# The first stage of a two-block transformer kernel: late convolutions re-ordered, ScalarE and VectorE work pinned behind evictions, the layer norm put between other products, and modulation products moved to the feed-forward stage

## The chip, the cores and the metric

One Trainium2 chip, the program on one core. The metric is the device time of one execution in microseconds (us), the median of three runs.

## What is computed

Two blocks over 512 tokens of width 1024, in float32 accuracy. Only the first stage of the first block, its layer norm and the start of its feed-forward part matter here:

```python
def first_block(x, ...):
        h = rmsnorm(x, norm1_g[l])
        z = h @ w_in[l] + b_in[l]
        z_glu, z_rx, z_rg, z_ga, z_gb = jnp.split(z, split_idx, axis=-1)

        u = z_glu[..., :D_CONV] * jax.nn.sigmoid(z_glu[..., D_CONV:])
        u = causal_depthwise_conv(u, conv_dw_w[l], conv_dw_b[l])     # 31 taps
        u = jax.nn.silu(layernorm(u, conv_ln_g[l], conv_ln_b[l]))
        y_a = u @ conv_w_out[l] + conv_b_out[l]

        xb = causal_depthwise_conv(z_rx, lru_conv_w[l], lru_conv_b[l])   # 4 taps
        hb = rg_lru(xb, lru_wa[l], lru_ba[l], lru_wx[l], lru_bx[l], lru_lambda[l])
        y_b = (hb * jax.nn.gelu(z_rg, approximate=True)) @ lru_w_out[l]

        m = jax.nn.sigmoid(z_ga) * y_a + jax.nn.sigmoid(z_gb) * y_b
        x = x + m @ w_mix_out[l]
        h = rmsnorm(x, norm2_g[l])
        x = x + (jax.nn.silu(h @ ffn_w1[l]) * (h @ ffn_w3[l])) @ ffn_w2[l]
```

Beside it a vector c is turned into 72 modulation columns for the second block, `silu(c) @ w_ada` (w_ada is 72 tiles of 128 x 1024).

## The kernel before

Activations lie channels on partitions, tokens along the free axis: a tensor of width 1024 is eight tiles of 128 x 512. **Products.** Every float32 operand is split in two (high and low part), and each K tile of a product is three matmuls, high x high, low x high, high x low (`mm3`, L132, L133, L134). A product of K = 1024 is 24 matmuls, one of K = 1280 is 30. Weights land by DMA from SyncE's queue in a ring of five `st` tiles; ScalarE copies a tile to `whi` (L125), VectorE, or GpSimd for some, subtracts it to `wlo` (L126); both have rings of five. Products land in a ring of three PSUM tiles `mm`, which must be evicted before the fourth product on starts; sums over partitions and convolution accumulators use a second PSUM ring of five, `ax`.

**Order of the work.** The program is a list of steps in one order, and every engine runs its instructions in the order in which the steps wrote them, save that a scheduler moves an instruction to where its inputs are expected. The first stage's steps are
g0 r0 r1 r2 r3 r4 g1 g2 a0 r5 a1 g3 a2 r6 a3 g4 a4 r7 r8 s0 g5 r9 b0 g6 b1 b2 g7 b3 b4 q0 q1 s1 q2 ... q9:
g are the gated-unit tiles (two products, `ga` evicted at L421 and `th` at L430 by ScalarE), r the recurrence's inputs, a and b its two gate products (`gt`, L545), s its scan, q the gelu gates (`ge`, then split to `hbh` and `hbl`). Then come eight pairs z_m, y_m (`yb_step`: a gate `thb` and a product over `hbh`), ga0 to ga7 (gates `tha`), ya0 to ya7 (products over the layer norm's output `u2h`, `u2l`) and the mixer's mx0 to mx7, and the feed-forward part.

g0 and r0 to r4 run before the normalised input is there: their products use the raw input, and VectorE multiplies the result by the norm's factor (`raw_z`, L395). What follows them, the 31-tap convolution of g0 and `rest` of r0 to r4 (three 4-tap products `xb`, L406, and a split to `xbh`, `xbl`), is kept in a list `late` and written when `norm_h(6)` has made the normalised input.

The 31-tap convolution is VectorE work in the background: taps d = 0 and 1 are ScalarE copies that start two PSUM accumulators (L401, L403, L404), the other 29 are VectorE multiply-adds (L406 `ax<-th,d_hdw,ax`); `total` joins the two (L446, L447), GpSimd adds up the channel sum `lnm` (L479). `later` queues such pieces in `bg` with a cost, `runbg` writes them after a step as far as that step's slack allows, and a NEXT mark ends its turn. The layer norm is queued the same way (`ln_push`): mean (L196, L224, L634), subtraction and squares (L639, L252), the inverse root (L232, L200 to L202, L217), output (L646, L647 and a split). What is still queued after ga7 is written there at once (`flush`).

An `ada_step` multiplies one w_ada tile with c and sums it up (VectorE, L327); its 512 KB come through the same `st` ring. Of the 72, 4 are written after y products, 8 after ga, 6 after ya, and the others during the first feed-forward part at a rate of 1.0 a product (`ada_between`).

`NKEEP` limits how many split weight tiles of a product are kept for its second token half.

Of the kernel before, what the change touches and what calls it, by code (L numbers as in the profile page):

```python
# [16 lines left out]
ALU = mybir.AluOpType  # L17
# [36 lines left out]
def build(tc, I, O, dbg=None):  # L54
# [11 lines left out]
    LA_D, LA_P = 4, 4  # L66
    NKEEP = {"w_mix_out": 3, "w_out": 3, "ffn_w2": 2}
    uid = [0]
# [263 lines left out]
    H = {}  # L332
# [30 lines left out]
    def behind(hold):  # L363
        return tc.issue_after(H["h_last"]) if hold else nullcontext()

    late = []

    def norm_h(m0):
        def fn(W):
            if m0 == 0:  # L370
                nc.gpsimd.dma_start(crow, I["c_2"].partition_broadcast(P))
                H["h"] = pairs(KT)
            ts = []
            for m in (m0, m0 + 1):
                t = at(n="ht")
                V.scalar_tensor_tensor(t, X[m], col("norm1_g", m), H["R"], ALU.mult, ALU.mult)
                act(H["h"][m][0], t, AF.Copy)
                ts.append(t)
            for m in (m0, m0 + 1):
                h, l = H["h"][m]  # L380
                H["h_last"] = V.tensor_tensor(l, ts[m - m0], h, ALU.subtract).ins
            if m0 + 2 == KT:
                for f in late:
                    f()
                late[:] = [None]
        return fn

    def raw_end(W):
        del H["xg"], H["R"]

    def raw_z(W, t):

        ps = pmm()
        gemm(ps, W, H["xg"])
        V.tensor_tensor(t, ps, H["R"], ALU.mult)  # L395
        return t
# [11 lines left out]
    CV = [None] * KT  # L408
    EV = [None]

    def glu_step(m, raw=False):
# [11 lines left out]
        def fg(W):  # L423
# [3 lines left out]
            else:  # L427
                pg = pmm()
                gemm(pg, W, H["h"])
            act(u, pg, AF.Tanh, bias=dcol["hb_in"][:, 8 + m:9 + m], scale=0.5)  # L430
            V.scalar_tensor_tensor(u, u, 1.0, st["a"], ALU.add, ALU.mult)
            cv = {}

            def taps(d0, d1):
                def f():
                    if d0 == 0:
                        cv["p"] = [pax(), pax()]
                    for d in range(d0, d1):
                        w = dcol["hdw"][:, m * 31 + 30 - d:m * 31 + 31 - d]
                        acc = cv["p"][d % 2]  # L440
                        delay(acc, u, d, w, col("conv_dw_b", m), first=d < 2)
                return f

            def total():
                CV[m] = at(n="cv")
                act(CV[m], cv["p"][0], AF.Copy)  # L446
                V.tensor_tensor(CV[m], CV[m], cv["p"][1], ALU.add)  # L447
# [37 lines left out]
    def rx_step(j, raw=False):  # L485
# [19 lines left out]
        def rest(z, xb, hold=False):  # L505
# [5 lines left out]
            def parts():  # L511
                XBP[j] = (at(F32R, "xbh"), at(F32R, "xbl"))
                split(xb, *XBP[j])

# [21 lines left out]
    def gate_step(g, m):  # L536
        j = g * 5 + m
        def fn(W):
            (hi, lo, kc), = W
            for q, nmq in ((0, "hba"), (1, "hbx")):  # L540
# [3 lines left out]
                th = at(n="gt")  # L544
                act(th, pg, AF.Tanh, bias=dcol[nmq][:, j:j + 1], scale=0.5)  # L545
                GT[q, j] = th
# [6 lines left out]
            V.scalar_tensor_tensor(tt, a2, 1.0, tt, ALU.add, ALU.mult)  # L553
            V.scalar_tensor_tensor(XB[j], ith, 1.0, XB[j], ALU.add, ALU.mult)
            GT[2, j] = tt
# [19 lines left out]
    def rg_step(j):  # L575
        def fn(W):
            pz = pmm()
            gemm(pz, W, H["h"])
            ge = at(n="ge")
            EV[0] = act(ge, pz, AF.Gelu_apprx_tanh, bias=col("b_in", 26 + j))  # L580
            V.tensor_tensor(ge, ge, XB[j], ALU.mult)

            def parts():
                HB[j] = (at(F32R, "hbh"), at(F32R, "hbl"))
                split(ge, *HB[j])
            defer(2, parts)
        add(wunits("w_in", 26 + j, KT, [8]), fn, own=1.4)

    pool_steps = [0, 0]
    for it in ("g0 r0 r1 r2 r3 r4 g1 g2 a0 r5 a1 g3 a2 r6 a3 g4 a4 r7 r8 s0 g5 r9 b0 g6 b1 b2 g7 b3 b4 "  # L590
               "q0 q1 s1 q2 q3 q4 q5 q6 q7 q8 q9").split():
        n = int(it[1])
        if it in ("g0", "r0", "r1", "r2", "r3", "r4"):
            {"g": glu_step, "r": rx_step}[it[0]](n, raw=True)
            if it in ("r1", "r2", "r3"):
                for m in {"r1": (0, 2), "r2": (4,), "r3": (6,)}[it]:
                    add([], norm_h(m), own=2.9 + (12.0 if m == 6 else 0.0))
            if it == "r4":
                pool_steps[0] = len(steps)
                add([], raw_end)  # L600
            continue
# [5 lines left out]
    def yb_step(m):  # L607
        st = {}

        def fz(W):  # L610
            pz = pmm()
            gemm(pz, W, H["h"])
            th = at(n="thb")
            act(th, pz, AF.Tanh, bias=dcol["hb_in"][:, 44 + m:45 + m], scale=0.5)
            st["th"] = th
# [8 lines left out]
        add(wunits("lru_w_out", m, NRNN, [5, 5]), fy, own=0.6)  # L624
        if m % 2:
            ada_step()

# [23 lines left out]
    def ln_push(W):  # L651
        bg.extend([NEXT, NEXT])
        later(0.9, ln_mean)
# [3 lines left out]
        for m in range(KT):  # L657
            later(1.4, lambda m=m: ln_out(m))

    for m in range(KT):  # L660
        yb_step(m)
# [5 lines left out]
    def ga_step(m):  # L667
        def fn(W):
            pz = pmm()
            gemm(pz, W, H["h"])  # L670
            TA[m] = at(n="tha")
            act(TA[m], pz, AF.Tanh, bias=dcol["hb_in"][:, 36 + m:37 + m], scale=0.5)
        add(wunits("w_in", 36 + m, KT, [8]), fn)
        ada_step()

    def ya_step(m):
# [11 lines left out]
        add(wunits("conv_w_out", m, KT, [8]), fn, own=2.1)  # L688
        if m < 6:
            ada_step()  # L690

# [225 lines left out]
    def ada_between():  # L917
        H["ada"] = H.get("ada", 0.0) + 1.0
        while H["ada"] >= 1.0:
# [695 lines left out]
    for i, (units, fn, slack) in enumerate(steps):  # L1615
# [16 lines left out]
        elif i < front[0]:  # L1632
            runbg(slack - spent[0])
        else:
# [83 lines left out]
```

## Time and profile before

| | |
|---|---|
| median of three runs | 2270.68 us (2270.66 to 2271.85) |
| profiled execution, its own time | 2268.78 us |
| its span, first to last instruction | 2267.1 us |
| mean granted TensorE clock | 0.991 |
| PE (TensorE) busy | 2207.7 us, 97% |
| DVE (VectorE) busy | 1401.8 us, 62% |
| ACT (ScalarE) busy | 941.8 us, 42% |
| POOL (GpSimd) busy | 159.3 us, 7% |

The profile is of one execution. "Idle before" a group is the time in which its engine did nothing, and after the arrow stands the instruction that ended it. The granted clock is 1.00 at 2.4 GHz and 0.50 at 1.2 GHz.

### The profile page before, as it was taken

The page shows a single profiled execution, that of the slowest core. Times are in us where ns is not written, and L with a number is a line of the kernel's source. Part 1 is how long each engine was busy: PE and PEld are TensorE (multiplying, and loading weights), DVE is VectorE, ACT ScalarE, POOL GpSimd, SP SyncE. Part 2 cuts the span into 40 slices and gives each one's busy share as a digit, 9 for nine tenths or more (in the row PEclk, how much of TensorE's full clock was granted, in tenths as well). Part 3 has the DMA queues.
Part 4 walks back from the last instruction along what each step waited for, and adds up shares of the span by engine and source line. Part 5 has one row for each costly group of instructions (what it writes and reads, how often), then busy time and mean ns, then how long its engine had stood idle before and what let it go on. Part 6 is the DMA issues. An engine that isn't in the chain of part 4 may idle for free.

```text
span 2267.1 us, 29984 instructions
## 1 busy us (share of the span) xinstructions
PE 2207.7 (97%) x11688; PEld 1888.2 (83%) x11688; DVE 1401.8 (62%) x2349; ACT 941.8 (42%) x1517; POOL 159.3 (7%) x179
## 2 busy tenths in 40 slices
PE   8899999699999999999999999999999999999997
PEld 6687788588888899988889987888888899988887
DVE  7999996768555448433325768675656558433334
ACT  6566433443222235322224567573433445322232
POOL 3334330000000000000100011000000000000000
PEclk9999999799999999999999999999999999999999
DMA  5433347245656534423234431213222323423342
GB/s 191 118 92 122 101 134 225 82 144 174 203 195 192 150 103 149 131 94 102 86 102 129 161 96 57 66 47 103 66 75 75 117 89 96 147 95 98 92 121 66
DMA packets 81438, 265.54 MB, mean 117 GB/s; under 512 B 10208, under 2 KB 12512, under 8 KB 81296
## 3 DMA queue, kind: packets, MB, share of 16 engines
q1 hardware_dynamic: 79888, 262.64, 36.8%
q8 instruction: 92, 1.51, 0.3%
q0 software_dynamic: 1264, 0.69, 0.1%
q14 instruction: 50, 0.41, 0.1%
q10 hardware_dynamic: 144, 0.29, 0.0%
HBM read 255.13 MB, written 4.19 MB: 114 GB/s over the span
## 4 chain that ended last, share of the span: by engine, by line
PE 81%; DVE 11%; issue 1%; ACT 1%; DMA 0%; POOL 0%; DVEq 0%; ACTq 0%; POOLq 0%
PE mm L132 24%; PE mm L133 24%; PE mm L134 24%; DVE ax L406 3%; DVE wlo L126 1%; PE ax L1231 1%; PE ax L1232 1%; PE ax L1233 1%; PE ax L1286 1%; PE ax L224 1%; PE ax L1415 1%; DVE xb L406 1%; PE ax L196 1%; DVE xb L567 1%; DMA st<-w_ada 0%
## 5 line engine op out<-in xcount | busy, mean ns | idle before, releaser
L125 ACT ACTIVATE whi<-st 128x1024 fp32r<-128x1024 f32 (+3 forms) x420 | 427.1, 1018 | 959.3 <-PE mm L133 594.4
L126 DVE TENSOR_TENSOR wlo<-st,whi 128x1024 fp32r<-128x1024 f32 (+3 forms) x378 | 454.1, 1202 | 415.8 <-ACT whi L125 414.7
L132 PE MATMUL mm<-pfh,whi 128*128 128x512 f32 (+1 forms) x1676 | 568.9, 339 | 0.5 <-ACT sq L251 0.5
L133 PE MATMUL mm<-pfl,whi 128*128 128x512 f32 (+1 forms) x1676 | 565.6, 338 | 0.0
L134 PE MATMUL mm<-pfh,wlo 128*128 128x512 f32 (+1 forms) x1676 | 564.4, 337 | 1.2 <-DVE wlo L126 1.2
L134 PEld LDWEIGHTS mm<-pfh,wlo 128*128 128x128 f32 x1676 | 316.8, 189 | 34.0 <-DVE wlo L126 1.9
L132 PEld LDWEIGHTS mm<-pfh,whi 128*128 128x128 f32 x1676 | 317.2, 189 | 33.5 <-ACT sq L251 1.4
L133 PEld LDWEIGHTS mm<-pfl,whi 128*128 128x128 f32 x1676 | 317.1, 189 | 31.7 <-issue 0.5
L132 PE MATMUL mm<-hi,whi 128*128 128x512 f32 x464 | 183.0, 394 | 10.4 <-ACT hi L354 6.2
L133 PE MATMUL mm<-lo,whi 128*128 128x512 f32 x464 | 183.4, 395 | 1.3 <-DVE lo L355 1.3
L134 PE MATMUL mm<-hi,wlo 128*128 128x512 f32 x464 | 182.4, 393 | 0.4 <-DVE wlo L126 0.4
L132 PE MATMUL mm<-mh,whi 128*128 128x256 f32 (+1 forms) x528 | 176.7, 335 | 2.2 <-ACT mh L852 1.1
L133 PE MATMUL mm<-ml,whi 128*128 128x256 f32 (+1 forms) x528 | 176.9, 336 | 0.0
L134 PE MATMUL mm<-mh,wlo 128*128 128x256 f32 (+1 forms) x528 | 176.4, 334 | 0.0
L406 DVE SCALAR_TENSOR_TENSOR ax<-th,d_hdw,ax 128x508 f32<-128x508 f32 (+27 forms) x232 | 157.7, 729 | 1.1 <-ACT ax L401 0.2
L133 PE MATMUL mm<-m1l,whi 128*128 128x512 f32 x368 | 143.3, 390 | 0.2 <-DVE m1l L686 0.2
L134 PE MATMUL mm<-m1h,wlo 128*128 128x512 f32 x368 | 143.0, 389 | 0.0
L132 PE MATMUL mm<-m1h,whi 128*128 128x512 f32 x368 | 143.0, 389 | 0.0
L327 DVE SCALAR_TENSOR_TENSOR st<-st,crow 128x1024 f32<-128x1024 f32 x72 | 88.5, 1229 | 73.6 <-DMA st<-w_ada 73.5
L865 DVE TENSOR_TENSOR fs<-fs,mm 128x512 f32<-128x512 f32 (+1 forms) x75 | 45.0, 600 | 128.0 <-PE mm L134 127.7
L132 PEld LDWEIGHTS mm<-hi,whi 128*128 128x128 f32 x464 | 88.1, 190 | 29.6 <-ACT hi L354 6.2
L132 PEld LDWEIGHTS mm<-mh,whi 128*128 128x128 f32 x528 | 100.1, 190 | 13.1 <-ACT mh L852 1.5
(363 smaller groups left out, 3319.2 us busy)
## 6 DMA issues: line engine op xcount, KB each, us to landing
st<-w_gu SPq DMA_DIRECT2D x102, 512.0 KB, 3.5
st<-w_ada SPq DMA_DIRECT2D x72, 512.0 KB, 4.0
st<-ffn_w SPq DMA_DIRECT2D x56, 512.0 KB, 3.6
st<-w_in SPq DMA_DIRECT2D x51, 512.0 KB, 4.0
st<-w2fm SPq DMA_DIRECT2D x51, 512.0 KB, 3.5
st<-w_dn SPq DMA_DIRECT2D x38, 448.0 KB, 3.3
st<-w_dn SPq DMA_DIRECT2D x24, 512.0 KB, 3.6
st<-w2v SPq DMA_DIRECT2D x16, 512.0 KB, 3.5
```

The source lines that it names most:

```text
L125: h = act(hi, src, AF.Copy)
L126: (eng or V).tensor_tensor(lo, src, hi, ALU.subtract)
L132: mm(out, whi, xh, start=start, stop=False)
L133: mm(out, whi, xl, start=False, stop=False)
L134: block[0] = mm(out, wlo, xh, start=False, stop=stop)
L196: mm(pc[:, i * nt + j:i * nt + j + 1], acc[:, r[0] + P * j:r[0] + P * (j + 1)], ones1, start=True, stop=True)
L224: mm(R[:, :nt * P], ones, dg.rearrange("p n t -> p (n t)"), start=True, stop=True)
L327: V.scalar_tensor_tensor(w, w, 1.0, crow, ALU.mult, ALU.mult, accum_out=mods[:, n:n + 1])
L406: V.scalar_tensor_tensor(acc[:, d:], u[:, :T - d], w, acc[:, d:], ALU.mult, ALU.add)
L567: V.tensor_tensor_scan(XB[j], GT[0, j], XB[j], 0.0, ALU.mult, ALU.add)
L865: V.tensor_tensor(s, s, rs(st["u"], r), ALU.mult)
L1231: mm(o, h[:, sl], hi[c], start=k == 0, stop=False)
```

## The change

1. `NKEEP` loses `w_mix_out` and has 8 instead of 3 for `w_out`, the product at the end of the second block's mixer.
2. `norm_h(6)` writes three late pieces (conv of g0, rest of r0, r1); those of r2, r3 and r4 are written in `raw_end`, behind r4's VectorE multiplication (`z_last`).
3. The convolution's ScalarE taps, `total` and the splits to `xbh` and `hbh` are pinned behind the last gate activation (`EV`), its VectorE taps behind the last gate multiplication but one (`DV`). `CV[m]` uses u's tile again. The last `hb` split is deferred by one step instead of two.
4. Stated costs: 5.0 instead of 12.0 for `norm_h(6)`, 7.0 for `raw_end`, a factor of 1.15 on the background from z0 on, and one NEXT less before the layer norm.
5. `ada_step`: none in the y and ga stages, 8 instead of 6 in ya, and 1.2 a product in the feed-forward part.

```diff
-    NKEEP = {"w_mix_out": 3, "w_out": 3, "ffn_w2": 2}
+    NKEEP = {"w_out": 8, "ffn_w2": 2}
...
+    NEARLY = 3
     late = []
...
             if m0 + 2 == KT:
-                for f in late:
+                for f in late[:NEARLY]:
                     f()
-                late[:] = [None]
+                del late[:NEARLY]
         return fn
 
     def raw_end(W):
         del H["xg"], H["R"]
+        H["h_last"] = H["z_last"]
+        for f in late:
+            f()
+        late[:] = [None]
 
     def raw_z(W, t):
...
-        V.tensor_tensor(t, ps, H["R"], ALU.mult)
+        H["z_last"] = V.tensor_tensor(t, ps, H["R"], ALU.mult).ins
         return t
...
+    DV = [None, None]
+
+    def behind_ev():
+        return tc.issue_after(EV[0].ins) if EV[0] is not None else nullcontext()
+
+    def behind_dv():
+        return tc.issue_after(DV[0].ins) if DV[0] is not None else nullcontext()
+
+    def dv(ins):
+        DV[:] = [DV[1], ins]
...
-            act(u, pg, AF.Tanh, bias=dcol["hb_in"][:, 8 + m:9 + m], scale=0.5)
-            V.scalar_tensor_tensor(u, u, 1.0, st["a"], ALU.add, ALU.mult)
+            EV[0] = act(u, pg, AF.Tanh, bias=dcol["hb_in"][:, 8 + m:9 + m], scale=0.5)
+            dv(V.scalar_tensor_tensor(u, u, 1.0, st["a"], ALU.add, ALU.mult))
...
-                        delay(acc, u, d, w, col("conv_dw_b", m), first=d < 2)
+                        with behind_ev() if d < 2 else behind_dv():
+                            delay(acc, u, d, w, col("conv_dw_b", m), first=d < 2)
...
-                CV[m] = at(n="cv")
-                act(CV[m], cv["p"][0], AF.Copy)
+                CV[m] = u
+                with behind_ev():
+                    act(u, cv["p"][0], AF.Copy)
...
-                split(xb, *XBP[j])
+                with behind_ev():
+                    act(XBP[j][0], xb, AF.Copy)
+                V.tensor_tensor(XBP[j][1], xb, XBP[j][0], ALU.subtract)
...
-            defer(2, parts)
+            defer(2 if j < NRNN - 1 else 1, parts)
...
-                    add([], norm_h(m), own=2.9 + (12.0 if m == 6 else 0.0))
+                    add([], norm_h(m), own=2.9 + (5.0 if m == 6 else 0.0))
             if it == "r4":
                 pool_steps[0] = len(steps)
-                add([], raw_end)
+                add([], raw_end, own=7.0)
...
         add(wunits("lru_w_out", m, NRNN, [5, 5]), fy, own=0.6)
-        if m % 2:
-            ada_step()
...
     def ln_push(W):
-        bg.extend([NEXT, NEXT])
+        bg.append(NEXT)
...
         add(wunits("w_in", 36 + m, KT, [8]), fn)
-        ada_step()
...
         add(wunits("conv_w_out", m, KT, [8]), fn, own=2.1)
-        if m < 6:
-            ada_step()
+        ada_step()
...
     def ada_between():
-        H["ada"] = H.get("ada", 0.0) + 1.0
+        H["ada"] = H.get("ada", 0.0) + 1.2
...
         elif i < front[0]:
-            runbg(slack - spent[0])
+            runbg((slack - spent[0]) * (1.15 if i >= yb0 else 1.0))
```

The built programs have the same number of instructions on every engine (PE 11378, DVE 2275, ACT 1442, POOL 179 rows, 571 DMAs on SP). The order differs at the places of points 2 to 5; of point 1 no row of any engine differs. Lines of the change are shifted by 5 to 19 against those of before (L395 is L400, L406 is L411, L421 is L436, L430 is L445, L634 is L653).

**VectorE around r4's multiplication** (`rx<-mm,R`, the eviction that frees r4's PSUM tile). `xb_355`, `xb_391`, `xb_460`, `xb_504` are the taps of r0 to r3. Before:

```order
L406 SCALAR_TENSOR_TENSOR xb_355<-rx_354,pcol,xb_355 128x509
L406 SCALAR_TENSOR_TENSOR xb_391<-rx_390,pcol,xb_391 128x509
L406 SCALAR_TENSOR_TENSOR xb_460<-rx_459,pcol,xb_460 128x511
L406 SCALAR_TENSOR_TENSOR xb_504<-rx_503,pcol,xb_504 128x511
L406 SCALAR_TENSOR_TENSOR xb_460<-rx_459,pcol,xb_460 128x510
L406 SCALAR_TENSOR_TENSOR xb_504<-rx_503,pcol,xb_504 128x510
L406 SCALAR_TENSOR_TENSOR xb_460<-rx_459,pcol,xb_460 128x509
L406 SCALAR_TENSOR_TENSOR xb_504<-rx_503,pcol,xb_504 128x509
L395 TENSOR_TENSOR rx_559<-mm_561,R_249 128x512
```

and now:

```order
L411 SCALAR_TENSOR_TENSOR xb_355<-rx_354,pcol,xb_355 128x509
L411 SCALAR_TENSOR_TENSOR xb_391<-rx_390,pcol,xb_391 128x509
L400 TENSOR_TENSOR rx_553<-mm_555,R_249 128x512
L411 SCALAR_TENSOR_TENSOR xb_460<-rx_459,pcol,xb_460 128x511
L411 SCALAR_TENSOR_TENSOR xb_504<-rx_503,pcol,xb_504 128x511
L411 SCALAR_TENSOR_TENSOR xb_460<-rx_459,pcol,xb_460 128x510
L411 SCALAR_TENSOR_TENSOR xb_504<-rx_503,pcol,xb_504 128x510
```

The six taps of r2 and r3 have gone from ahead of the eviction to behind it.

**ScalarE around the evictions of g1 and g2** (`ga`, `th`) and the first gate a0 (`gt`). Before:

```order
L421 ACTIVATE ga_619<-mm_620,pcol 128x512
L125 ACTIVATE whi_749<-st_557 128x1024
L125 ACTIVATE xbh_670<-xb_560 128x512
L125 ACTIVATE whi_787<-st_596 128x1024
L430 ACTIVATE th_674<-mm_675,d_hb_in 128x512
L401 ACTIVATE ax_1047<-th_674,pcol,d_hdw 128x512
L421 ACTIVATE ga_720<-mm_721,pcol 128x512
L430 ACTIVATE th_755<-mm_756,d_hb_in 128x512
L545 ACTIVATE gt_800<-mm_793,d_hba 128x512
```

and now:

```order
L436 ACTIVATE ga_611<-mm_612,pcol 128x512
L531 ACTIVATE xbh_650<-xb_460 128x512
L125 ACTIVATE whi_690<-st_501 128x512
L531 ACTIVATE xbh_654<-xb_504 128x512
L531 ACTIVATE xbh_658<-xb_554 128x512
L445 ACTIVATE th_662<-mm_663,d_hb_in 128x512
L125 ACTIVATE whi_749<-st_551 128x1024
L125 ACTIVATE whi_787<-st_596 128x1024
L436 ACTIVATE ga_720<-mm_721,pcol 128x512
L445 ACTIVATE th_755<-mm_756,d_hb_in 128x512
L564 ACTIVATE gt_800<-mm_793,d_hba 128x512
```

g1's `th` stands ahead of the two weight copies now, and the first tap of g1's convolution (L401) no longer stands ahead of g2's `ga`. The same kind of move is at b1: on VectorE the three taps of r9 (`xb_1392` before, `xb_1391` now), behind which ScalarE's split and the `ga` of g6 queue, were mixed with seven convolution taps, and now follow one another 26 rows earlier.

**The layer norm's mean.** VectorE at the end of the convolutions before, in the ga stage (`st,mods` is an `ada_step`, `cv<-cv,ax` the last convolution's total):

```order
L327 SCALAR_TENSOR_TENSOR st_3437,mods<-st_3437,crow 128x1024
L126 TENSOR_TENSOR wlo_3399<-st_3209,whi_3398 128x1024
L327 SCALAR_TENSOR_TENSOR st_3479,mods<-st_3479,crow 128x1024
L126 TENSOR_TENSOR wlo_3441<-st_3252,whi_3440 128x1024
L447 TENSOR_TENSOR cv_3241<-cv_3241,ax_2949 128x512
L634 TENSOR_SCALAR s_3286<-ax_3281 128x4
```

there, now:

```order
L411 SCALAR_TENSOR_TENSOR ax_2857<-th_1675,d_hdw,ax_2857 128x482
L126 TENSOR_TENSOR wlo_3047<-st_2917,whi_3046 128x1024
L464 TENSOR_TENSOR th_1675<-th_1675,ax_2858 128x512
L126 TENSOR_TENSOR wlo_3083<-st_2967,whi_3082 128x1024
L653 TENSOR_SCALAR s_3120<-ax_3115 128x4
L217 TENSOR_TENSOR dg_3122<-ident,s_3120 128x512
```

and TensorE now, where the mean's sums (L196) and its broadcast (L224) stand at the end of ga3 (`mm_3088`) and in ga4 (`mm_3151`):

```order
L134 MATMUL mm_3088<-hi_435,wlo_2960 128x512
L196 MATMUL ax_3115<-ones,lnm_1593 128x1 x4
L132 MATMUL mm_3151<-hi_421,whi_2963 128x512
L133 MATMUL mm_3151<-lo_422,whi_2963 128x512
L134 MATMUL mm_3151<-hi_421,wlo_2964 128x512
L132 MATMUL mm_3151<-hi_423,whi_2963 128x512
L133 MATMUL mm_3151<-lo_424,whi_2963 128x512
L134 MATMUL mm_3151<-hi_423,wlo_2964 128x512
L132 MATMUL mm_3151<-hi_425,whi_2963 128x512
L224 MATMUL ax_3124<-dg_3122,ones 128x512
```

Before, all four of the norm's statistics products (two L196, two L224) stood alone behind ga7's last matmul. Now the squares' sums stand behind 13 matmuls of ga6, the second broadcast 13 matmuls later, behind 2 of ga7, and the 22 others of ga7 stand between it and the first product over `u2h`. On ScalarE the table load for Silu moves from the copy of c (L326, in q9) to the first layer norm output (L647, now L666); both programs have 14 table loads.

## Rows read from the trace of the kernel before

**Rows 1.** The waits of TensorE over the first 460 us: who waited <- for what: us in total, times, longest us.

```profile
PE ax L196 <- DVE lnv L252: 9.7, 1, 9.7
...
PE mm L132 <- ACT ga L421: 5.0, 2, 2.8
```

**Rows 2.** Busy time of each engine in a stretch of 50 us (PE, PEld, DVE, ACT, POOL with instructions), then the granted clock, the DMA share and GB/s.

```profile
300.00:350.00 50.00, 50.00 (x222) 41.42 (x221) 47.78 (x68) 15.73 (x21) 14.12 (x9) 1.00 0.51 163
```

**Rows 3.** TensorE's timeline, the instructions that had to wait in the first stage: start us, us, engine, line, operation, out<-in, and in brackets the idle time before with what ended it.

```profile
67.74 0.73 PE L132 MATMUL mm<-hi,whi 128*128 128x512 f32 x1 [3.75 <-DVE rx L395]
...
82.00 0.50 PE L132 MATMUL mm<-xbh,whi 128*128 128x512 f32 x1 [1.50 <-ACT th L430]
...
85.86 0.50 PE L132 MATMUL mm<-xbh,whi 128*128 128x512 f32 x1 [2.19 <-ACT ga L421]
...
176.64 0.50 PE L132 MATMUL mm<-xbh,whi 128*128 128x512 f32 x1 [2.77 <-ACT ga L421]
...
267.40 0.50 PE L133 MATMUL mm<-hbl,whi 128*128 128x512 f32 x1 [2.26 <-DVE hbl L126]
```

**Rows 4.** VectorE's timeline ahead of the first of these waits.

```profile
55.89 11.20 DVE L406 SCALAR_TENSOR_TENSOR xb<-rx,pcol,xb 128x511 f32<-128x511 f32 x12
67.01 0.68 DVE L395 TENSOR_TENSOR rx<-mm,R 128x512 f32<-128x512 f32 x1
```

**Rows 5.** Three stretches in the columns of rows 2: behind the waits at 67.74, at 176.64 and through the layer norm.

```profile
67.80:71.20 3.40, 3.40 (x8) 2.68 (x9) 3.32 (x6) 3.40 (x7) 0.00 (x0) 0.51 0.00 0
...
177.10:180.50 3.40, 3.40 (x10) 2.62 (x9) 3.40 (x6) 3.37 (x8) 2.97 (x3) 0.50 0.80 160
...
402.40:426.20 23.80, 8.69 (x21) 6.10 (x22) 18.59 (x40) 11.85 (x20) 0.00 (x0) 0.50 0.06 22
```

**Rows 6.** ScalarE's timeline ahead of the waits at 85.86 and at 176.64.

```profile
84.42 0.78 ACT L401 ACTIVATE ax<-th,pcol,d_hdw 128x512 f32<-128x512 f32 x1 [2.47 <-DVE th L431]
85.14 0.67 ACT L421 ACTIVATE ga<-mm,pcol 128x512 f32<-128x512 f32 x1
...
174.44 0.63 ACT L125 ACTIVATE xbh<-xb 128x512 fp32r<-128x512 f32 x1 [9.09 <-DVE xb L406]
174.98 1.04 ACT L125 ACTIVATE whi<-st 128x1024 fp32r<-128x1024 f32 x1
175.92 0.67 ACT L421 ACTIVATE ga<-mm,pcol 128x512 f32<-128x512 f32 x1
```

**Rows 7.** TensorE's timeline: the first matmuls of ga0 (353.67), of ga4 (375.43) and of mx0 (467.32), and between the last two the layer norm's statistics products and the first product over its output.

```profile
353.67 0.39 PE L132 MATMUL mm<-hi,whi 128*128 128x512 f32 x1
...
375.43 0.39 PE L132 MATMUL mm<-hi,whi 128*128 128x512 f32 x1
...
398.59 1.05 PE L196 MATMUL ax<-ones,lnm 128*128 128x1 f32 x8 [1.23 <-POOL lnm L479]
...
400.62 1.13 PE L224 MATMUL ax<-dg,ones 128*128 128x512 f32 x2 [0.98 <-DVE dg L217]
...
411.40 1.84 PE L196 MATMUL ax<-ones,lnv 128*128 128x1 f32 x8 [9.66 <-DVE lnv L252]
...
416.49 2.05 PE L224 MATMUL ax<-dg,ones 128*128 128x512 f32 x2 [3.25 <-DVE dg L217]
...
421.39 1.65 PE L132 MATMUL mm<-u2h,whi 128*128 128x512 f32 x3 [2.85 <-ACT u2h L125]
...
467.32 0.39 PE L132 MATMUL mm<-m1h,whi 128*128 128x512 f32 x1
```

**Rows 8.** The same two kinds of statistics product at the program's start, with no wait before them.

```profile
17.41 1.02 PE L196 MATMUL ax<-ones,acc 128*128 128x1 f32 x8
...
23.62 1.12 PE L224 MATMUL ax<-dg,ones 128*128 128x512 f32 x2
```

**Rows 9.** VectorE's timeline: five taps on two accumulators in turn, five on one accumulator, and the end of the convolutions, with GpSimd's channel sum behind it.

```profile
257.83 3.29 DVE L406 SCALAR_TENSOR_TENSOR ax<-th,d_hdw,ax 128x497 f32<-128x497 f32 x5
...
339.97 3.82 DVE L406 SCALAR_TENSOR_TENSOR ax<-th,d_hdw,ax 128x497 f32<-128x497 f32 x5
...
394.15 1.23 DVE L327 SCALAR_TENSOR_TENSOR st<-st,crow 128x1024 f32<-128x1024 f32 x1 [2.54 <-DMA st<-w_ada]
...
396.44 0.68 DVE L447 TENSOR_TENSOR cv<-cv,ax 128x512 f32<-128x512 f32 x1
...
397.27 1.27 POOL L479 TENSOR_TENSOR lnm<-lnm,cv 128x512 f32<-128x512 f32 x1 [27.63 <-DVE cv L447]
```

**Rows 10.** VectorE's groups up to 396.6 us: line, operation, xcount | busy us, mean ns of one | idle before.

```profile
L406 DVE SCALAR_TENSOR_TENSOR ax<-th,d_hdw,ax 128x508 f32<-128x508 f32 (+27 forms) x232 | 157.7, 729 | 1.1 <-ACT ax L401 0.2
L126 DVE TENSOR_TENSOR wlo<-st,whi 128x1024 fp32r<-128x1024 f32 (+2 forms) x41 | 50.5, 1236 | 0.6 <-ACT whi L125 0.5
...
L327 DVE SCALAR_TENSOR_TENSOR st<-st,crow 128x1024 f32<-128x1024 f32 x18 | 22.4, 1244 | 23.9 <-DMA st<-w_ada 23.9
```

**Rows 11.** ScalarE's timeline around a table load.

```profile
144.78 1.28 ACT L564 ACT_TABLE_LOAD   x1
146.07 2.20 ACT L564 ACTIVATE tt<-tt 128x512 f32<-128x512 f32 x4
```

**Rows 12.** ScalarE's weight copies from 480 to 800 us, in the columns of rows 10.

```profile
L125 ACT ACTIVATE whi<-st 128x1024 fp32r<-128x1024 f32 (+1 forms) x59 | 61.8, 1047 | 197.8 <-PE mm L133 105.5 <-issue 92.3
```

**Rows 13.** The transfers of the modulation tiles over the program: xcount, KB each, us from issue to landing.

```profile
st<-w_ada SPq DMA_DIRECT2D x72, 512.0 KB, 4.0
```

More of the change, by code (lines that the diff above doesn't have):

```diff
@@ L544, in fn @@
                 th = at(n="gt")
-                act(th, pg, AF.Tanh, bias=dcol[nmq][:, j:j + 1], scale=0.5)
+                EV[0] = act(th, pg, AF.Tanh, bias=dcol[nmq][:, j:j + 1], scale=0.5)
                 GT[q, j] = th
@@ L553, in fn @@
             V.scalar_tensor_tensor(tt, a2, 1.0, tt, ALU.add, ALU.mult)
-            V.scalar_tensor_tensor(XB[j], ith, 1.0, XB[j], ALU.add, ALU.mult)
+            dv(V.scalar_tensor_tensor(XB[j], ith, 1.0, XB[j], ALU.add, ALU.mult))
             GT[2, j] = tt
@@ L580, in fn @@
             EV[0] = act(ge, pz, AF.Gelu_apprx_tanh, bias=col("b_in", 26 + j))
-            V.tensor_tensor(ge, ge, XB[j], ALU.mult)
+            dv(V.tensor_tensor(ge, ge, XB[j], ALU.mult))
             def parts():
                 HB[j] = (at(F32R, "hbh"), at(F32R, "hbl"))
-                split(ge, *HB[j])
-            defer(2, parts)
+                with behind_ev():
+                    act(HB[j][0], ge, AF.Copy)
+                V.tensor_tensor(HB[j][1], ge, HB[j][0], ALU.subtract)
+            defer(2 if j < NRNN - 1 else 1, parts)
         add(wunits("w_in", 26 + j, KT, [8]), fn, own=1.4)
@@ L613, in fz @@
             th = at(n="thb")
-            act(th, pz, AF.Tanh, bias=dcol["hb_in"][:, 44 + m:45 + m], scale=0.5)
+            EV[0] = act(th, pz, AF.Tanh, bias=dcol["hb_in"][:, 44 + m:45 + m], scale=0.5)
             st["th"] = th
@@ L658, in ln_push @@
             later(1.4, lambda m=m: ln_out(m))
+    yb0 = len(steps)
     for m in range(KT):
@@ L671, in fn @@
             TA[m] = at(n="tha")
-            act(TA[m], pz, AF.Tanh, bias=dcol["hb_in"][:, 36 + m:37 + m], scale=0.5)
+            EV[0] = act(TA[m], pz, AF.Tanh, bias=dcol["hb_in"][:, 36 + m:37 + m], scale=0.5)
         add(wunits("w_in", 36 + m, KT, [8]), fn)
-        ada_step()
     def ya_step(m):
```

## The prediction

> **What bounds the kernel now.** I first read the waits of TensorE, since it is busy nearly all the time: over the first 460 us its longest waits are for the layer norm's squares and for evictions of `ga` [rows 1]. The windows then show the steady state next to them: from 300 to 350 us TensorE never pauses, and VectorE is at 47.8 of 50 us beside it [rows 2]. So the first stage has two limits, TensorE as the bound and VectorE close behind; what an edit is worth is what it takes from TensorE's waits. Third, its timeline gives each wait with its releaser: five in the first stage [rows 3], five more in the layer norm [rows 7]. Fourth, the windows behind the longest ones show what a pause costs beyond itself: 3.4 us at a granted clock of 0.51 and of 0.50 after the waits of 3.75 and 2.77, and 23.8 us at 0.50 through the layer norm [rows 5].
>
> At full clock a matmul of 512 columns takes (375.43 - 353.67) / 96 = 0.2267 us [rows 7], a product of 24 5.44.
>
> **The change, part by part.**
>
> *r4's eviction.* g2's first product waits 3.75 us for r4's tile [rows 3]. Its eviction starts at 67.01, behind twelve taps that took 11.20 [rows 4]. Six of these now stand behind it: 5.6 us earlier, more than the wait, so it goes, and with it the half clock, (1 - 0.51) x 3.40 = 1.7 [rows 5]. The six taps are late next; r2 and r3 are wanted at a0 only. **5.4 saved.**
>
> *a0.* Two waits, 1.50 and 2.19 [rows 3]. The second is for g2's `ga` at 85.14, behind a convolution tap that itself waited 2.47 for VectorE [rows 6]; the tap has gone from there, and g1's `th` stands ahead of two weight copies. What stays is `ga` behind one such copy: I leave one eviction, 0.7 (0.67 [rows 6]). 3.7 - 0.7 = **3.0 saved**; bounds 0 and 3.7.
>
> *b1.* The wait of 2.77 [rows 3] is for g6's `ga`, behind a split of r9's `xb` for which ScalarE idled 9.09 until VectorE's tap was done [rows 6]. Those taps stood among seven convolution taps, 7 x 0.64 = 4.5, and now stand ahead. 2.77 and half of 3.40 at half clock [rows 5] are 4.5; again I leave 0.7. **3.8 saved**; bounds 0 and 4.5.
>
> *y0.* 2.26 for the last `hbl` [rows 3]: its split comes a step earlier, a whole product ahead. **2.3 saved.**
>
> *The layer norm.* From ga4's first matmul to mx0's are 467.32 - 375.43 = 91.9 us [rows 7]. Twelve products lie in it, 288 x 0.2267 = 65.3. The statistics products now stand between other matmuls. They last 1.02 and 1.12 where nothing waits [rows 8]; about 0.2 of each is drain that the next matmul covers (a matmul lasts 0.39 and takes 0.2267 [rows 7]), so two of each are 2 x (1.02 + 1.12) - 4 x 0.2 = 3.5. The rest, 23.1, is waiting and half clock, and goes where each chain has cover:
>
> - The mean stands at ga3's end, so the convolutions must end there. VectorE no longer does the modulation products of these stages, 1.24 each and waiting 23.9 us for their tiles over 18 of them [rows 10]. By the order it now has 116 taps between the first y gate and the mean, at 0.64 with two accumulators in turn ((3.29 - 0.73) / 4 [rows 9]; the last one takes its whole duration, 0.729 [rows 10]): 74.2; 14 splits at 1.24 [rows 10] are 17.4; 13 evictions and totals at 0.68 [rows 9] 8.8: 100.4. TensorE has 475 matmuls there, 107.7. At the tail, from the last y product on, 20 taps (12.8), 5 splits (6.2) and GpSimd's 1.27 [rows 9] make 20.3 against four products, 21.8. Margin 1.5 us, no wait.
> - From the squares' sums to the second broadcast is a wait of 3.25 now [rows 7]; 13 matmuls, 2.95, cover it: 0.3 left.
> - From that broadcast to the first product over `u2h` are 421.39 - 416.49 = 4.90, half clock included [rows 7]; the cover is 22 matmuls, 4.99. The next tiles come from ScalarE and VectorE at nearly TensorE's pace: up to 1.1 left.
>
> With 0.2 for the squares, 1.6 stays. 91.9 - 65.3 - 3.5 - 1.6 = **21.5 saved**.
>
> Here a table load is new: Silu's stands ahead of the first layer norm output. The load of the rows lasts 1.28, and the activation behind it starts 0.01 after it [rows 11]. It needs no tile, so ScalarE can run it while VectorE multiplies: nothing, or 1.28 if it is held until the tile is there, which the 1.6 above nearly holds. The Trainium skill, "ScalarE: Activation LUTs", section "What ACT_TABLE_LOAD costs", speaks against this part: a switch costs a load of 1283 ns and a drain of about 1380 ns, 2.66 us together. The load's length agrees; rows 11 show no drain behind it. By the rule the chain would be 1.4 longer and the forecast 2236 instead of 2235. I go by the row.
>
> *The moved modulation products.* Ten leave for the feed-forward part (18 before the mixer, now 8). There the weight copies idle 105.5 us for TensorE to free a tile [rows 12], so tiles land long before they are wanted; VectorE has room for 1.24 more in one product of five. I cost them at nothing, covered by that; without that cover, see the third rival. In ya one product each is 1.24 in 5.44.
>
> *Kept weight tiles.* No row of the order differs for it: nothing. GpSimd's and SP's instructions are the same in number; pinned copies on ScalarE cost no time of their own, but hold what is behind them (second rival).
>
> **Sum:** 5.4 + 3.0 + 3.8 + 2.3 + 21.5 = 36.0. The profiled execution is 2268.8 us, so 2232.8; the median of the runs shown is 1.9 above it: 2234.7, said as **2235**. A measurement of this kernel can tell about 0.2%, 4.5 us, from no change.
>
> **The rivals.**
>
> *VectorE is late at the mean.* The margin of 1.5 us is an estimate. Convolution taps of one accumulator in a row take 0.77 ((3.82 - 0.73) / 4 [rows 9]): if half of the 116 did, 58 x 0.13 = 7.5 more, and TensorE, with the mean's sums ahead of ga4 in its order, would wait about 6 of it and lose 1.7 to 3.4 at half clock [rows 5]: some 2243, at worst 2252 if the squares wait as well, as 9.66 did [rows 7]. For it: VectorE at 47.8 of 50 [rows 2], and 42 taps, 27 us, more behind the first y gate than before (116 instead of 74 by the order). Against: the modulation products' 22.4 busy and 23.9 idle [rows 10] leave the same stretch.
>
> *ScalarE holds evictions.* A split or a first tap pinned behind an eviction still waits for VectorE with later evictions behind it; then the a0 and b1 waits stay: 3.7 + 4.5 - 1.4 = 6.8 less saved, 2241. For it: the 9.09 of idle at 174.44 [rows 6] are this very thing. Against: the order shows taps behind `ga`, and r9's `xb` earlier.
>
> *Transfers in the feed-forward part, slower than before.* If the five-tile ring has no room for a fifth more tiles, each moved one delays the weight tile behind it by its landing, 4.0 [rows 13], and its product 1.24: 10 x 5.2 = 52, 2286. It decides from where ScalarE's copies there wait for a DMA instead of TensorE; it needs over 36 us to end above 2270, seven of the ten exposed. Against: the 105.5 us [rows 12].
>
> *The change does not do what it says.* For the kept tiles that is so, at a price of 0; for the rest the order shows the moves. If ScalarE's and VectorE's waits merely moved elsewhere in the first stage, only the layer norm's 21.5 would be saved: 2249.
>
> **How the numbers follow.** The forecast has 0.62 (its own range is 2229, with none of the 3.0 that I left and some small waits gone too, to 2238, by the bounds of a0 or b1 alone), VectorE late 0.16, ScalarE holding 0.12, the first stage's gains lost 0.03, transfers 0.04 for slower, and 0.03 that such losses together leave it within 0.2%. The range from 2229 to 2250 takes in the first two rivals but for their worst ends. Faster by over 0.2%: 0.62 + 0.16 + 0.12 + 0.03 = 0.93, said as 0.92; within 0.2% 0.03; slower 0.05, with a hundredth for a slowdown that I don't see.
>
> **What would show it.** Right: TensorE's timeline has no wait for r4's eviction, none over 1 us at a0, b1 and y0, and no half clock at 67 and 177; the mean's sums start without a wait at the end of ga3; from ga4 to mx0 are about 70 us at full clock; in the feed-forward part TensorE stays without pauses. Wrong: a wait of several us at the mean's or the squares' sums (VectorE late); `ga` or `th` as releasers at a0 or b1 (ScalarE holding); waits for `whi` or `wlo`, released by a DMA, between 480 and 800 us (transfers). If the part from ga4 to mx0 is over 80 us, the largest term has failed.

## The result

The change runs in 2234.8 us (median of four, 2233.64 to 2235.49), the kernel before beside it in 2271.26: a ratio of 0.9839, 95% interval 0.9822 to 0.9856. The forecast was 2235, range 2229 to 2250. The profiled execution took 2235.49, its span is 2233.8, the mean granted clock 0.997.

TensorE's waits of the change from 60 to 460 us (who waited, for what, total, times, longest), which answer to [rows 1] and [rows 3]:

```profile
PE mm L132 <- ACT m1h L704: 1.7, 2, 1.1
PE mm L132 <- ACT gt L564: 0.9, 1, 0.9
PE mm L133 <- DVE m1l L705: 0.6, 1, 0.6
PE mm L133 <- DVE u2l L126: 0.2, 1, 0.2
```

None of before's five is left. Two are new: 0.9 for a gate at b2, and 2.2 for the last `m1` tiles at mx0. TensorE's timeline (start us, us, engine, line, operation, out<-in) at products that end terms of the sum, at the statistics products and at the new waits:

```profile
69.18 0.39 PE L132 MATMUL mm<-hi,whi 128*128 128x512 f32 x1
...
74.62 0.39 PE L132 MATMUL mm<-xbh,whi 128*128 128x512 f32 x1
76.28 0.50 PE L132 MATMUL mm<-xbh,whi 128*128 128x512 f32 x1
...
167.20 0.50 PE L132 MATMUL mm<-xbh,whi 128*128 128x512 f32 x1 [0.86 <-ACT gt L564]
...
359.10 0.95 PE L196 MATMUL ax<-ones,lnm 128*128 128x1 f32 x8
361.62 1.02 PE L224 MATMUL ax<-dg,ones 128*128 128x512 f32 x2
374.88 1.02 PE L196 MATMUL ax<-ones,lnv 128*128 128x1 f32 x8
379.06 1.12 PE L224 MATMUL ax<-dg,ones 128*128 128x512 f32 x2
385.05 0.39 PE L132 MATMUL mm<-u2h,whi 128*128 128x512 f32 x1
...
429.54 0.39 PE L132 MATMUL mm<-m1h,whi 128*128 128x512 f32 x1
434.89 0.50 PE L132 MATMUL mm<-m1h,whi 128*128 128x512 f32 x1 [1.11 <-ACT m1h L704]
435.96 0.50 PE L133 MATMUL mm<-m1l,whi 128*128 128x512 f32 x1 [0.57 <-DVE m1l L705]
437.95 0.73 PE L132 MATMUL mm<-m1h,whi 128*128 128x512 f32 x2 [0.56 <-ACT m1h L704]
```

The four statistics products have no bracket: nothing was waited for. From ga3's end to mx0's first matmul are 429.54 - 359.10 = 70.44 us, against 467.32 - 375.43 = 91.89 in [rows 7]; each holds the norm's four statistics products and the twelve products of ga4 to ya7. The windows say the same of the clock (columns of [rows 2]); before, three such stretches stood at half clock [rows 5]:

```profile
67.80:71.20 3.40, 3.40 (x16) 2.81 (x15) 3.40 (x4) 1.21 (x3) 2.13 (x3) 1.00 0.38 82
177.10:180.50 3.40, 3.40 (x17) 2.81 (x16) 3.40 (x5) 0.90 (x1) 0.00 (x0) 1.00 0.04 17
...
359.10:429.54 70.44, 70.02 (x310) 56.30 (x309) 59.17 (x97) 38.45 (x54) 0.00 (x0) 1.00 0.51 171
```

### The profile page after: what moved, and what is told of

It reads as the page before. It is cut to its first block, busy times and chain, and to the rows that moved or that the text cites. A ratio compares the mean times of both kernels' runs of the same rounds, so it can differ in the third digit from the quotient of the medians.

```text
span 2233.8 us, 29966 instructions
## 1 busy us (share of the span) xinstructions
PE 2201.6 (99%) x11688; PEld 1884.6 (84%) x11688; DVE 1400.2 (63%) x2349; ACT 940.8 (42%) x1517; POOL 156.5 (7%) x179
## 4 chain that ended last, share of the span: by engine, by line
PE 89%; DVE 6%; ACT 2%; issue 1%; DMA 1%; DVEq 0%; SPq 0%; ACTq 0%
PE mm L132 27%; PE mm L133 27%; PE mm L134 26%; PE ax L1249 1%; PE ax L1250 1%; PE ax L1251 1%; DVE wlo L126 1%; PE ax L1304 1%; PE ax L224 1%; PE ax L1433 1%; PE ax L196 1%; DMA st<-w_ada 0%; ACT whi L125 0%; ACT p L1417 0%; DVE s L1416 0%
## 5 line engine op out<-in xcount | busy, mean ns | idle before, releaser
L126 DVE TENSOR_TENSOR wlo<-st,whi 128x1024 fp32r<-128x1024 f32 (+2 forms) x378 | 454.5, 1204 | 372.3 <-ACT whi L125 371.5
L411 DVE SCALAR_TENSOR_TENSOR ax<-th,d_hdw,ax 128x510 f32<-128x510 f32 (+28 forms) x232 | 154.2, 729 | 0.0
L134 PEld LDWEIGHTS mm<-mh,wlo 128*128 128x128 f32 x528 | 100.9, 191 | 10.2
```

The lines of the kernel that those rows point to most:

```text
L126: (eng or V).tensor_tensor(lo, src, hi, ALU.subtract)
L134: block[0] = mm(out, wlo, xh, start=False, stop=stop)
L411: V.scalar_tensor_tensor(acc[:, d:], u[:, :T - d], w, acc[:, d:], ALU.mult, ALU.add)
```

## The experiments

Each was timed in five rounds. Before ran at 2272.2 to 2272.5 beside them, so the change would stand at 0.9839 x 2272.2 = 2235.7 there; "worth" below is against that. The intervals are some 3 to 4 us to each side, so by its time alone a run is told from the change from about 5 us on; below that the traces have to show it. All edits are to the changed kernel, but for the fourth.

| run | us | ratio to before, 95% |
|---|---|---|
| x1_ya6 | 2240.51 | 0.9859 (0.9846 to 0.9872) |
| x4_adaback | 2250.34 | 0.9905 (0.9890 to 0.9920) |
| x5_lnback | 2254.12 | 0.9918 (0.9904 to 0.9931) |
| x7_adaonly | 2269.18 | 0.9987 (0.9978 to 0.9996) |
| x2_late5 | 2244.59 | 0.9877 (0.9861 to 0.9893) |
| x3_nopins | 2251.56 | 0.9910 (0.9896 to 0.9924) |
| x3b_noev | 2247.23 | 0.9886 (0.9872 to 0.9899) |
| x3c_nodv | 2238.19 | 0.9847 (0.9833 to 0.9860) |
| x6_hb | 2235.08 | 0.9840 (0.9826 to 0.9853) |
| x8_noya | 2236.95 | 0.9843 (0.9829 to 0.9857) |
| x10_mixA | 2234.68 | 0.9836 (0.9822 to 0.9849) |
| x11_early | 2257.24 | 0.9931 (0.9918 to 0.9943) |

**The layer norm.** Where the modulation products are:

```diff
+        if m % 2:                  # y
+            ada_step()
+        ada_step()                 # ga
-        ada_step()                 # ya
+        if m < 6:
+            ada_step()
-        H["ada"] = H.get("ada", 0.0) + 1.2
+        H["ada"] = H.get("ada", 0.0) + 1.0
```

> The changed kernel with all modulation products where they were before (four after y products, eight after ga, six after ya, 1.0 a product in the feed-forward part); the rest of the change stays. By the order the mean's sums then stand behind ga4 instead of ga3, and the squares' sums and the second broadcast behind the last matmul of ga7. Theory A: VectorE's time and its waits for w_ada tiles are what kept the layer norm late, so the move is a condition of the largest term: squares' sums, second broadcast and first u2h are exposed again (about 10 to 16 us with the half clock), less the 2.2 at mx0: 2243 to 2249. Rival: the first stage's other edits alone bring the norm early, and the modulation move is worth nothing: 2233 to 2236.

2250.3, 14.6 slower, just above theory A's span. The second broadcast alone waited 12.87 us, the first `u2h` 2.85, and 20.48 us ran at half clock. TensorE's timeline at ga4's first matmul, at the two waits and at mx0's first matmul:

```profile
358.96 0.39 PE L132 MATMUL mm<-hi,whi 128*128 128x512 f32 x1
...
396.49 2.07 PE L224 MATMUL ax<-dg,ones 128*128 128x512 f32 x2 [12.87 <-DVE dg L217]
401.41 1.65 PE L132 MATMUL mm<-u2h,whi 128*128 128x512 f32 x3 [2.85 <-ACT u2h L125]
...
447.32 0.39 PE L132 MATMUL mm<-m1h,whi 128*128 128x512 f32 x1
```

From ga4 to mx0 are 447.32 - 358.96 = 88.36 us: 17.9 more than in the change, 3.5 less than before. Some 2.9 come back behind it, since mx0 waits for nothing here. The edit moves two things at once, VectorE's work and, as the expectation says, the statistics in TensorE's order; no run brings the modulation products back and leaves the statistics where the change has them.

```diff
-        bg.append(NEXT)
+        bg.extend([NEXT, NEXT])
-            runbg((slack - spent[0]) * (1.15 if i >= yb0 else 1.0))
+            runbg(slack - spent[0])
```

> The changed kernel with the background's factor of 1.15 and the missing NEXT undone; all else as in the change. By the order the mean stands behind ga6, the squares' sums and the second broadcast behind ga7's last matmul. Theory A: the layer norm's gain hangs on where the statistics stand in TensorE's order. VectorE has then the same work, but the chain mean, subtraction, squares (about 10 us), root, broadcast, output runs against one product instead of four: 14 to 18 us of waits and half clock, 2249 to 2253. Rival: the gain is VectorE's lighter load, wherever the products stand: under 2240.

2254.1, 18.4 slower, theory A, 1.1 above its span. The same places of its timeline:

```profile
359.62 0.39 PE L132 MATMUL mm<-hi,whi 128*128 128x512 f32 x1
...
391.39 1.84 PE L196 MATMUL ax<-ones,lnv 128*128 128x1 f32 x8 [8.04 <-DVE lnv L252]
400.54 2.04 PE L224 MATMUL ax<-dg,ones 128*128 128x512 f32 x2 [7.31 <-DVE dg L217]
405.44 1.65 PE L132 MATMUL mm<-u2h,whi 128*128 128x512 f32 x3 [2.85 <-ACT u2h L125]
...
451.61 0.39 PE L132 MATMUL mm<-m1h,whi 128*128 128x512 f32 x1
```

From ga4 to mx0 are 91.99 us, as long as before: nothing of the layer norm's gain is left. So the place of the statistics in TensorE's order is a condition, and a lighter VectorE alone does not do it. Part 5 alone, on the kernel before:

> The kernel before with part 5 of the change alone (modulation products moved). By the order the mean stands behind ga6 and the squares' sums and second broadcast behind ga7. Theory A: the first stage's waits (about 16 us) stay, the layer norm saves only the mean's and part of the squares' waits, 3 to 6 us, and mx0 loses 2.2: 2267 to 2270. Rival (the modulation products were what held the norm): nearly the whole 21 us of the norm is saved, 2252 or less.

2269.2, 3.1 saved, inside theory A's span. Its layer norm takes 89.03 us from ga4 (378.41) to mx0 (467.44), 2.9 less than before. But the 2.2 that it was to lose at mx0 did not come: with the same eight modulation products in ya, mx0 waits for nothing here, nor in x5_lnback. And everything but those two:

```diff
+ both edits above: x4_adaback and x5_lnback together
```

> The changed kernel with parts 4 and 5 undone where they touch the layer norm (modulation products where they were, 1.0 a product, two NEXT, no 1.15): only the early re-ordering, the costs and the pins stay. By the order all four statistics products stand behind ga7 again. Theory A: the early terms and the layer norm's are separate, so 16 us are saved and the layer norm costs what it did: 2255 to 2257 where before is 2272. Rival: the pins push 42 convolution taps, 27 us, behind the y gates, and with the modulation products back VectorE ends the convolutions later than before: the mean waits longer, 2260 to 2270.

2257.2: 15.3 saved by the early terms alone (theory A 16), and the layer norm waits as before, 19.8 us in sum against 18.0. TensorE's waits from 60 to 800 us:

```profile
PE ax L196 <- DVE lnv L252: 11.6, 1, 11.6
PE ax L224 <- DVE dg L217: 5.4, 2, 3.3
PE mm L132 <- ACT u2h L125: 2.9, 1, 2.9
PE mm L132 <- ACT gt L564: 0.9, 1, 0.9
```

The early terms stand by themselves: ga4 starts at 359.26 here and ga3 ends at 359.10 in the change, against 375.43 before. The two edits of the layer norm do not add up: its 21.5 us shrink to 3.5 without the one (x4_adaback) and to nothing without the other (x5_lnback). The totals show 14.6 and 18.4 because the waits at mx0 go with it.

**r4's eviction.**

```diff
-    NEARLY = 3
+    NEARLY = 5
```

> The changed kernel with five late pieces instead of three written in norm_h(6) (conv of g0 and the taps of r0 to r3), so that the six taps of r2 and r3 stand ahead of r4's eviction on VectorE again, as before the change; r4's own stay behind it. Theory A: g2's first product waits for that eviction again, 3.75 us and half of 3.4 at half clock: 5.4 more, 2240. Rival: the pins and the lighter ScalarE have made room and the wait was only moved, so the taps matter little: 2235 to 2236.

2244.6, 8.9 and not 5.4. The wait of 3.75 is back to the hundredth; a0 also waits again, 2.02 for `th`, with another 3.41 us at half clock. A late eviction delays what queues behind it too.

**The pins.**

```diff
     def behind_ev():
-        return tc.issue_after(EV[0].ins) if EV[0] is not None else nullcontext()
+        return nullcontext()
     def behind_dv():
-        return tc.issue_after(DV[0].ins) if DV[0] is not None else nullcontext()
+        return nullcontext()
```

> The changed kernel without the pins (the convolution's taps, total and the splits to xbh and hbh are free again, neither behind the last gate activation nor behind the last gate multiplication). Theory A: the pins made the a0 and b1 terms; their waits come back, 3.9 and 3.5 measured between the two profiles, 2238 to 2242. Rival: the step order and the late list made these terms, since they decide when the taps are ready; the pins are worth under 1 us: 2234 to 2236.

2251.6, 15.9 slower: above both spans, and more than the two terms. Without the pins the re-ordered stage waits longer than before did, 3.15 at a0, 4.98 at b1 and 2.84 in the q products. ScalarE's timeline ahead of the second is that of [rows 6], only worse:

```profile
171.50 0.63 ACT L531 ACTIVATE xbh<-xb 128x512 fp32r<-128x512 f32 x1 [11.30 <-DVE xb L411]
172.04 1.04 ACT L125 ACTIVATE whi<-st 128x1024 fp32r<-128x1024 f32 x1
172.99 0.67 ACT L436 ACTIVATE ga<-mm,pcol 128x512 f32<-128x512 f32 x1
```

ScalarE idles 11.30 before a split whose `xb` is not there, with the eviction that TensorE wants behind it. One kind of pin at a time:

> The changed kernel without the pins behind the last gate activation (ScalarE's taps, total's copy and the splits to xbh and hbh are free), those of VectorE's taps stay. Without either the time was 2251.6. Theory A: the waits are ScalarE standing before a tap or a copy whose input VectorE has not ready, so the ScalarE pins make nearly all of the 16 us: 2248 to 2252. Rival: VectorE's taps ahead of the recurrence's taps are what makes the inputs late, and the VectorE pins make it: 2236 to 2239.

> The changed kernel without the pins of VectorE's taps behind the last gate multiplication but one; those of ScalarE stay. Theory A (ScalarE's pins make the 16 us): 2236 to 2240. Rival (VectorE's make it): 2248 to 2252. If both this and the run without ScalarE's pins lose most of it, neither pin is enough alone.

2247.2 and 2238.2: 11.5 and 2.5 slower. Theory A, though the first is a little under its span; the second is too small to tell by the times. In the traces ga4's first matmul, at 359.90 in the change, stands 9.9 us later without ScalarE's pins (369.82), 1.8 without VectorE's (361.72) and 17.4 without both (377.33). So ScalarE's pins carry most, and one kind makes up for a part of the other.

**y0.**

```diff
-            defer(2 if j < NRNN - 1 else 1, parts)
+            defer(2, parts)
```

> The changed kernel with the last hb split deferred by two steps again. Theory A: y0's last K tile waits for hbl again, 2.26 before: 2237. Rival: VectorE is less behind there now, and the split is ready in time either way: 2234.8.

2235.1: the times could hardly tell 2.3 us, but the trace has no wait at y0. The earlier split is worth nothing, theory A fell: in that run `hbl` is done 3 us before y0's last K tile wants it, where TensorE waited 2.26 for it before. So VectorE is less behind there. Part 5 is not the cause: alone it leaves a wait of 2.28. Nor do the pins show as one: without ScalarE's or without VectorE's y0 waits for nothing, without both 0.29, though TensorE comes later to y0 in these runs. The re-ordering and its costs are left, but no run singles them out.

**mx0 and the feed-forward part.** VectorE in the change, ahead of the last `ya` tiles:

```profile
427.87 1.23 DVE L327 SCALAR_TENSOR_TENSOR st<-st,crow 128x1024 f32<-128x1024 f32 x1 [0.79 <-DMA st<-w_ada]
...
429.02 0.69 DVE L701 SCALAR_TENSOR_TENSOR ya<-tha,ya 128x512 f32<-128x512 f32 x1
```

A modulation product waits for its tile, and the step of ya5 that leads to `m1h` and `m1l` stands behind it. That product starts 1.7 us ahead of mx0's first matmul (429.54). In x5_lnback and x7_adaonly, where mx0 waits for nothing, ya's last modulation product starts 7.3 and 7.8 us ahead of it (451.61 and 467.44):

```profile
444.34 1.23 DVE L327 SCALAR_TENSOR_TENSOR st<-st,crow 128x1024 f32<-128x1024 f32 x1 [0.54 <-DMA st<-w_ada]
...
459.63 1.23 DVE L327 SCALAR_TENSOR_TENSOR st<-st,crow 128x1024 f32<-128x1024 f32 x1
```

So the products in ya cost something only together with the early layer norm; why they come so late there stays open.

```diff
-        ada_step()
+        if m < 6:
+            ada_step()
-        H["ada"] = H.get("ada", 0.0) + 1.2
+        H["ada"] = H.get("ada", 0.0) + 1.25
```

> The changed kernel, with modulation products only after the first six ya products again (as before the change); the two that this frees go to the feed-forward part, at 1.25 a product instead of 1.2. Theory A: the three new waits at mx0 in the profile of the change (1.11, 0.57 and 0.56 us, all for the last ya tiles' m1h and m1l) come from the two modulation products that now stand in VectorE's order ahead of ya5's and ya6's last steps. Then they shrink to the 0.2 of the kernel before, and the time falls by about 2.0 to 2232.8. Rival: the waits come from ya0 and ya1 running interleaved and so ending late, or from ScalarE's weight copies; then the waits stay and the time is 2234.8, or higher by what the feed-forward part loses.

Half of each. The waits at mx0 fall from 2.24 to 0.68, but the time is 2240.5, 4.8 higher, and the trace shows why: the feed-forward part waits 5.5 us at 1.25 a product and not at all at 1.2. VectorE's timeline of this run, and the matmul that waited:

```profile
664.77 1.22 DVE L327 SCALAR_TENSOR_TENSOR st<-st,crow 128x1024 f32<-128x1024 f32 x1 [3.67 <-DMA st<-w_ada]
...
665.92 0.68 DVE L884 TENSOR_TENSOR fs<-fs,mm 128x512 f32<-128x512 f32 x1
```

```profile
666.65 0.50 PE L132 MATMUL mm<-m1h,whi 128*128 128x512 f32 x1 [2.02 <-DVE fs L884]
```

VectorE waits 3.67 for a modulation tile, with an eviction behind it. How near to this the change itself is, the idle time of ScalarE before its splits behind that eviction shows (6.5 us in the kernel before); in the change, and then in this run, from 450 to 800 us (xcount | busy, mean ns | idle before):

```profile
L125 ACT ACTIVATE pfh<-fs 128x512 fp32r<-128x512 f32 x19 | 12.0, 634 | 77.4 <-DVE fs L883 77.4
```

```profile
L125 ACT ACTIVATE pfh<-fs 128x512 fp32r<-128x512 f32 x19 | 12.0, 633 | 126.4 <-DVE fs L884 126.4
```

77.4 / 19 = 4.1 us a product in the change, 6.7 here, 0.3 before. TensorE waits for nothing at the first and 5.5 us at the second: the PSUM ring covers the one and not the other.

```diff
-        ada_step()                 # ya: none
-        H["ada"] = H.get("ada", 0.0) + 1.2
+        H["ada"] = H.get("ada", 0.0) + 1.6
```

> The changed kernel with no modulation product after ya products at all: all eight go to the feed-forward part too, at 1.6 a product instead of 1.2. Theory A: the feed-forward part has room in its tile ring, so nothing is lost there, and the waits at mx0 go: 2232.5. Rival (the forecast's third): 1.6 tiles a product leave the weight tiles late, each extra modulation tile exposes some of its 4.0 landing and 1.24 product: 2240 to 2275, with waits for whi or wlo between 450 and 650 us.

2237.0: not to be told from the change. The waits at mx0 are down to 0.2, and 3.6 us of waits for the same eviction, with 3.4 us at half clock, take their place. So the loss is not in proportion to the rate: TensorE waited 5.5 us for that eviction at 1.25, 3.6 at 1.6. That it hangs on which tiles fall together is a guess; no run shows it.

```diff
-        ada_step()                 # ya
+        if m < 6:
+            ada_step()
-            if 1 < m < 6:          # mixer
+            if 0 < m < 7:
                 ada_step()
```

> The changed kernel with modulation products after the first six ya products alone; the two that this frees go behind mixer products (after mx1 to mx6 instead of mx2 to mx5), and the feed-forward part keeps 1.2 a product. Theory A: with ya's last two gone the waits at mx0 shrink from 2.2 to the 0.7 that the run with 1.25 a product showed, and the mixer has room on VectorE, so nothing comes back: 1.5 below the changed kernel, at a ratio to before of 0.983 (2233 to 2234 where before is 2272). Rival: an eviction in the mixer waits behind a multiplication that waits for its tile, as in the feed-forward part at 1.25 a product: 1 to 4 us above the changed kernel.

2234.7, ratio 0.9836: no difference from the change, but the waits at mx0 did not shrink as theory A had it. (Four of the 72 modulation products stand behind mx2 to mx5 in the change, and in the kernel before too.) One modulation product came to stand ahead of ya7's last steps on VectorE, waiting for its tile, and mx0 waits 2.39 for `m1h` in one piece, with 3.41 us at half clock behind it in the profiled execution. No version that I ran is clearly faster than the change.

## Why the prediction was right

Each term, as the difference of start times between the two profiles at the products that bound it (forecast beside it):

- r4's eviction, to g2's second product: 74.91 - 69.18 less 0.09 from the start, 5.6 (5.4). Undone: 8.9.
- a0, to r5: 3.9 (3.0). The 0.7 that I left did not stay: the second gate waited 0.14.
- a4, to r8: 0.7, a small wait of 0.37 that I left out.
- b1, to g7: 3.5 (3.8). Its wait went; 0.9 came at b2.
- y0: 2.5 (2.3). The size was right, the cause was not: the earlier split is worth nothing.
- The layer norm, to mx0: 21.45 (21.5). Statistics sums and broadcasts waited for nothing, `u2l` 0.2. Up to the first `u2h` the statistics cost 385.05 - 359.10 - 96 x 0.2267 = 4.2 where I had taken 3.5, and what is left behind it is 1.0 and not 1.6: the two errors cancel.
- The moved modulation products: forecast at nothing, they cost 2.6 at mx0. Here my sum failed: I counted VectorE's time in ya, and not that the last two stand ahead of the chain `ya`, `m1h`, `m1l` when the layer norm is early. Where it is late, they cost nothing.
- Later: 1.9 lost between mx3 and the end: 1.5 of clock at 1848 us (below), 0.6 behind the last product, 0.3 gained near 855 us. The first feed-forward part, where the modulation products went, lost nothing.

These make 33.3 us between the spans of two single executions; between the medians it is 36.5, since the profiled execution of before was 2.5 under its median and that of the change 0.7 over. That 36.0 hit the second so closely is partly luck: the terms of the first stage and the layer norm were each right within 1 us, 1.7 us that I had left out there stand against the overlooked 2.6, and single executions of one kernel differ by 2 to 5.

Two rivals were near. *VectorE late at the mean*: the margin was not 1.5 us but 0.3. VectorE's first tap of the tail and GpSimd's last channel sum, in the change:

```profile
338.55 3.31 DVE L411 SCALAR_TENSOR_TENSOR ax<-th,d_hdw,ax 128x501 f32<-128x501 f32 x5
...
356.65 2.14 POOL L496 TENSOR_TENSOR lnm<-lnm,th 128x512 f32<-128x512 f32 x1 [26.53 <-DVE th L464]
```

The channel sum ends at 358.79, the statistics sums start at 359.10. The tail took 20.24 us, as estimated (20.3). But VectorE enters it 1.2 us behind ga0's first matmul, at 337.34, and that the estimate left out. The channel sum took 2.14 and not the 1.27 of [rows 9] while VectorE subtracted two SBUF tiles beside it (356.42 to 357.64). The Trainium skill, "SBUF — State Buffer", section "SBUF: two separate sides", has it that such a pair of operations shuts each other out whole; the 0.87 more agrees with an overlap of 1.0. *ScalarE holds evictions* is what the stage does without the pins: 11.30 of idle before a split. *Transfers* exist from 1.25 a product on, but through VectorE: the forecast looked for late `whi` or `wlo`, and what is late is the eviction behind a modulation product.

The table load lies where the order put it, while ScalarE waits for VectorE, and the first output starts 0.59 after the load's end, released by VectorE:

```profile
379.50 1.28 ACT L666 ACT_TABLE_LOAD   x1
381.37 1.52 ACT L666 ACTIVATE th<-th,pcol 128x512 f32<-128x512 f32 x2 [0.59 <-DVE th L665]
```

The drain of 1380 ns that the Trainium skill's "ScalarE: Activation LUTs", section "What ACT_TABLE_LOAD costs", states would have ended later than that start: no row shows it.

## What to carry to other kernels

An in-order engine that serves two users needs its waiting work behind the evictions, not only less of it: with the pins the early re-ordering saves 15 us, and taking ScalarE's away costs 11.5. Where a chain of statistics runs beside products, look at two things: the inputs in time, and the statistics matmuls several products ahead of their use. A lighter VectorE alone kept none of the 21 us (2.9 on the kernel before); with the load back, 3.5 were left, but there the matmuls had moved too. A filler (here a modulation product) that waits for a DMA is not free where its engine is idle: count what stands behind it.

## What the runs showed of the hardware

The same wait does not always cost clock. In the second block, the kernel before and the change have the same waits of 0.8 and 1.1 us (1879 and 1844 us); then, first before and then the change:

```profile
1883.30:1886.70 3.40, 3.40 (x31) 3.40 (x30) 3.40 (x10) 1.82 (x4) 0.00 (x0) 1.00 0.00 0
```

```profile
1848.30:1851.70 3.40, 3.40 (x18) 3.40 (x17) 3.40 (x10) 1.81 (x4) 0.00 (x0) 0.50 0.00 0
```

Of the twelve runs' profiles two had none there, six 3.4 and four 6.8 us at half clock: 0, 1.7 or 3.4 us on one unchanged place. Differences of that size between two single executions say nothing.
